# A hybrid encoder trunk on one core: the first mixer's projections read their stationary operand at a step of 8 or 16 bytes

## The chip, the core and the metric

The kernel runs on one core of a Trainium2 chip. A core has a matrix engine (TensorE, in the profile PE, with its weight loads as PEld), a vector engine (DVE), a scalar engine (ACT), GpSimd (POOL), and DMA queues, of which the one on SyncE (SP) carries most loads here. The on-chip memory SBUF has 128 partitions; a tile is 128 partitions by some elements of a row. Matmul results land in PSUM. The metric is the device time of one execution in microseconds. Three runs of the kernel before gave 1371.38, 1371.97 and 1373.08, so the median is 1371.97 us.

## The reference

The input x has 512 tokens of 1024 channels, in float32. Two layers follow each other; each has a token mixer and a gated feed-forward part with a convolution, both between RMS norms. Layer 0's mixer, which the change touches, has one input projection that feeds two groups of heads, retention and neighbourhood attention:

```python
def retention_na_mixer(hn, w_in, ...):
    proj = hn @ w_in
    R, N = RET_WIDTH, NA_WIDTH          # 512, 512
    rq, rk, rv, rg, nq, nk, nv = jnp.split(proj, [R, 2*R, 3*R, 4*R, 4*R + N, 4*R + 2*N], axis=-1)
    ...
    return jnp.concatenate([ret_out, na_out], axis=-1) @ w_out
```

`hn` is 512 x 1024 and `w_in` 1024 x 3584. Layer 1's mixer is a state-space scan (`ssd_mixer`) and is not touched, nor are the two feed-forward parts.

## The kernel before

**Products in three parts.** Each float32 product is made of three matmuls on fp32r operands. ACT rounds an operand to its high part (line 107), DVE subtracts it from the original to get the low part (line 108), and `mm3` adds high x high, high x low and low x high in PSUM (lines 116 to 118). In a row such as `mm<-xh,wlo`, the tile before the comma is the moving operand and the one behind it the stationary operand.

**The first mixer's projections.** `mixer0` walks over four pairs of heads. For each pair, the table `PAIRS` lists the steps; the five steps rq, rk, nq, nk and rg are projections, which go through `project` (the function inside `mixer0`, lines 711 to 733) to `proj_fm` (line 127). The result is feature-major: 128 features of the pair on the partitions, 512 tokens along the row. The stationary operand is therefore a piece of the weight, 128 input channels by 128 features, and the moving operand is `xh` or `xl`, 128 input channels by 512 tokens. One projection runs over KD = 8 key tiles of 128 input channels, so it has 8 x 3 = 24 products, and the four pairs have 4 x 5 x 24 = 480.

**The weights' way.** `wunit` (line 83) fetches one projection's weights as a tile of 128 x 1024 float32 with one DMA of 512 KB on SP (line 76), and casts and subtracts it as a whole. The host lays the array out beforehand: `_cols` (line 1340) puts, for partition p, the eight key tiles one behind the other, 128 features each. `wunit` hands the high and the low tile on as two halves of 512 columns, and `proj_fm` takes key tile k as the 128 neighbouring columns from k % 4 * 128 in half k // 4. `proj_fm` is used by the second mixer's projections too.

**The order around it.** The scheduler keeps the program's order on each engine, and lifts the weight casts ahead of it. On PE, pair 0's five projections come first, in one run. Pair p + 1's projections are then woven into pair p's attention steps, which are short matmuls: scores of 256 moving columns (lines 780, 781, 831, 832), transposes of 128 columns (lines 756, 848), states (line 766) and values (lines 793, 797, 858). Pair 1's projections thus start among pair 0's score matmuls and end ahead of pair 1's key transpose (line 756).

**Two other places that the prediction reads.** In the second mixer, line 1122 has matmuls of 128 moving columns that follow each other with a fresh stationary tile each. Line 985 is a copy on ACT from PSUM into the tile `etot`, 128 x 64 x 4, whose view `p h (i c) -> p c i h` has the 64 heads h innermost; a step from one h to the next is four elements, 16 bytes. Line 1004 is a copy of the same size into `tok`, where h is contiguous.

Of the kernel before, what the change touches and what calls it, by code (L numbers as in the profile page):

```python
# [17 lines left out]
P = 128  # L18
S = 512
NT = S // P  # L20
D = 1024
KD = D // P
# [8 lines left out]
class Env:  # L31
# [92 lines left out]
                self.tc.add_manual_dep(m.ins, i.ins.name, mybir.DependencyInfo(  # L124
                    mybir.DependencyClass.Sync, mybir.DependencyReason.DATA))

    def proj_fm(self, out, w, c0=0, c1=S):

        for k in range(KD):
            hi, lo = w[k // 4]  # L130
            c = slice(k % 4 * P, k % 4 * P + P)
            self.mm3(out[:, c0:c1], hi[:, c], lo[:, c],
                     self.xh[:, k, c0:c1], self.xl[:, k, c0:c1], k == 0, k == KD - 1)

# [436 lines left out]
def log1p_exp_neg(E, alloc, z):  # L571

    nc = E.nc
    e, s, q, r = (alloc(n) for n in "esqr")
    nc.vector.scalar_tensor_tensor(e, z, -1.0, z, op0=ALU.mult, op1=ALU.min)
    nc.scalar.activation(e, e, AF.Exp)
    nc.vector.tensor_scalar(s, e, 2.0, None, op0=ALU.add)
    nc.vector.reciprocal(s, s)
    nc.vector.tensor_tensor(s, s, e, op=ALU.mult)
    nc.vector.tensor_tensor(q, s, s, op=ALU.mult)  # L580
    nc.vector.tensor_scalar(r, q, 2.0 / 15, 2.0 / 13, op0=ALU.mult, op1=ALU.add)
    for c in (11, 9, 7, 5, 3, 1):
        nc.vector.tensor_tensor(r, r, q, op=ALU.mult)
        nc.vector.tensor_scalar(r, r, 2.0 / c, None, op0=ALU.add)
    nc.vector.tensor_tensor(r, r, s, op=ALU.mult)
    return r


NPAIR = 4
CH = 2 * P  # L590
TOEP = CH + P

# [14 lines left out]
def mixer0(E, w0, w_v, w_fm, tabs, dist_d, logit, gn, bias, w_out, g_post_row, done):  # L607
# [4 lines left out]
    with ExitStack() as ctx:  # L612
# [16 lines left out]
        zg = one.tile([P, 104], F32, name="zg")  # L629
        z, gnt = zg[:, :24], zg[:, 24:24 + NPAIR]  # L630
        nc.sync.dma_start(zg[:, :16], logit.partition_broadcast(P))
        nc.sync.dma_start(zg[:, 16:24 + NPAIR], gn)
        lp = log1p_exp_neg(E, lambda n: one.tile([P, 24], F32, name="lp_" + n), z)
# [13 lines left out]
        for s in range(2):  # L647
            ps = [E.mm.tile([P, 512], F32, name="mm") for _ in range(NT)]
            for u in range(4):
                w = w0.pop(0) if w0 else E.wunit(w_v[s, u])  # L650
                for t in range(NT):
                    tt = slice(t * P, (t + 1) * P)
                    for i in range(2):
                        k = 2 * u + i
# [56 lines left out]
        def project(p, o, nm):  # L711
            i = ("rk", "rq", "rg", "nq", "nk").index(nm)
            w = E.wunit(w_fm[i, p])
            ps = E.mm.tile([P, S], F32, name="mm")
            E.proj_fm(ps, w)
            if i < 2:
                a = E.tmp.tile([P, S], F32, name="ra", tag="tmp")
                b = E.tmp.tile([P, S], F32, name="rb", tag="tmp")
                nc.scalar.activation(a, ps, AF.Copy, scale=1.0 if i else 0.125)
                for j in range(4):  # L720
                    nc.sync.dma_start(b[32 * j:32 * j + 32], a[32 * (j ^ 1):32 * (j ^ 1) + 32])
                nc.gpsimd.tensor_tensor(b, b, rot[:, 1], op=ALU.mult)
                nc.vector.tensor_tensor(a, a, rot[:, 0], op=ALU.mult)
                nc.vector.tensor_tensor(a, a, b, op=ALU.add)
                o[nm] = (twice if i else stack)(nm, a)
                o[nm + "a"] = a
            elif i == 2:
                o[nm] = two.tile([P, S], F32, name=nm)
                nc.scalar.activation(o[nm], ps, AF.Silu)
            elif i == 3:  # L730
                o[nm] = stack(nm, ps.rearrange("p (r b c) -> p b r c", r=8, b=4))
            else:
                o[nm] = twice(nm, ps, 0.125)

        def decays(p, o):
# [11 lines left out]
            for c in range(2):  # L747
                cc = slice(c * CH, c * CH + CH)
                nc.scalar.activation(o["qs"][:, cc], away[:, cc], AF.Exp, scale=lgp[:, 2 * p + 1 - c:2 * p + 2 - c])
# [20 lines left out]
        def ret_scores(p, o, i):  # L770

            o["sd", i] = []
            cc = slice(i * P, i * P + CH)
            for h in range(2):
                ps = E.px.tile([P, 2, CH], F32, name="sc", tag="px")
                m = sd.tile([P, 2, CH], F32, name="sd", tag="sd")
                qt, ql = o["rq"]
# [4 lines left out]
                for j in range(2):  # L782
                    w = nc.vector.tensor_tensor(m[:, j], ps[:, j], o["toep"][h][:, P - j * P:P - j * P + CH], op=ALU.mult)
                o["sd", i].append((m, w))
# [77 lines left out]

        os = [{} for _ in range(NPAIR)]
        for p in range(NPAIR):
            for step in PAIRS[p].split():
                q = p + (step[0] == "+")
                step = step.strip("+")
# [472 lines left out]
def _cols(w):  # L1340

    f = w.shape[1]
    return w.reshape(KD, P, f // P, P).transpose(2, 1, 0, 3).reshape(f // P, P, 1024)


def _rows(w, order=None):

    k, n = w.shape
    w = w.reshape(k // P, P, n // 512, 512)
    if order is not None:  # L1350
        w = w[list(order)]
    return w.reshape(k // 256, 2, P, n // 512, 512).transpose(3, 0, 2, 1, 4).reshape(n // 512, k // 256, P, 1024)
# [9 lines left out]
def _rotary_tables(np):  # L1362
    half = 32
    inv = np.float32(1.0) / np.float32(10000.0) ** (np.arange(half, dtype=np.float32) / np.float32(half))
    ang = np.arange(S, dtype=np.float32)[:, None] * inv[None].astype(np.float32)
    c, s = np.cos(ang).T.astype(np.float32), np.sin(ang).T.astype(np.float32)
    return np.stack([np.concatenate([c, c, c, c]), np.concatenate([-s, s, -s, s])], 1)
# [18 lines left out]
def _layouts(np, i):  # L1386
    a = {"x": i["x"][0]}
    a["norms"] = np.stack([i[n] for n in ("norm_mix_pre", "norm_mix_post", "norm_ffn_pre", "norm_ffn_post")], 1)
    w = i["ab_w_in"][0]
    c = lambda j: w[:, 512 * j:512 * j + 512]  # L1390
    a["ab_v"] = np.stack([_rows(c(2))[0], _rows(c(6))[0]])
    a["ab_fm"] = np.stack([_cols(c(j)) for j in (1, 0, 3, 4, 5)])
    a["ab_rot"] = _rotary_tables(np)
    n, t, q = (np.arange(m, dtype=np.float32) for m in (P, S, TOEP))
    k = n[:, None] + P * np.arange(NT, dtype=np.float32)
    a["ab_dist"] = np.concatenate([q[None] - P - n[:, None], np.tile(np.where(t < CH, CH - t, t - CH + 1), (P, 1)),
                                   np.where(k < CH, CH - 1 - k, k - CH)], 1).astype(np.float32)
    logit = i["ab_ret_decay_logit"][0].reshape(2, 8)
    a["ab_logit"] = logit.reshape(16)
    zp = np.repeat(logit.reshape(2, NPAIR, 2).transpose(2, 1, 0).reshape(2, 2 * NPAIR), 64, 0)  # L1400
    a["ab_gn"] = np.concatenate([zp, i["ab_ret_gn_g"][0].reshape(NPAIR, P).T], 1)
    a["ab_bias"] = _na_bias(np, i["ab_na_rpb"][0])
    a["ab_out"] = _rows(i["ab_w_out"][0], OUT_ORDER)

    w = i["c_w_in"][0]
    wz, wx, wb, wc, wd = w[:, :2048], w[:, 2048:4096], w[:, 4096:4608], w[:, 4608:5120], w[:, 5120:]
    a["c_dt"] = wd.reshape(KD, P, 2 * SSD_H).transpose(1, 0, 2).reshape(P, 512)
    a["c_fm"] = np.stack([np.concatenate([_cols(wb[:, P * g:P * g + P]), _cols(wc[:, P * g:P * g + P]),
                                          _cols(wx[:, 512 * g:512 * g + 512]), _cols(wz[:, 512 * g:512 * g + 512])])
                          for g in range(NG)])  # L1410
    cw = np.concatenate([i["c_conv_w"][0], i["c_conv_b"][0][None]])
    xw, bw, cw = cw[:, :2048].reshape(6, NG, 4, P), cw[:, 2048:2560].reshape(6, NG, 1, P), cw[:, 2560:].reshape(6, NG, 1, P)
    a["c_cw"] = np.concatenate([bw, cw, xw], 2).transpose(3, 1, 2, 0)
    sign = np.repeat(np.array([-1, 1], np.float32), SSD_H)
    a["c_dtc"] = np.tile(np.stack([i["c_dt_bias"][0].reshape(-1), i["c_a_log"][0].reshape(-1), sign], 1), (2, 1))
    d = np.repeat(i["c_d_skip"][0].reshape(4 * NG, 2), 64, 1)
    a["c_cols"] = np.stack([d.T, i["c_norm_g"][0].reshape(4 * NG, P).T], 1)
    a["c_mask"] = np.triu(np.ones((P, P), np.float32))
    a["c_out"] = np.stack([_rows(i["c_w_out"][0][512 * g:512 * g + 512]) for g in range(NG)])

    for l in range(2):
        w = i["ffn_w_up"][l]
        a[f"f{l}_up"] = np.stack([_cols(w[:, s * FFN:(s + 1) * FFN]) for s in range(2)])
        cw = np.concatenate([i["ffn_conv_w"][l], i["ffn_conv_b"][l][None]])
        a[f"f{l}_cw"] = cw.reshape(4, 2, NF, P).transpose(3, 1, 2, 0)
        a[f"f{l}_down"] = _quarters(np, i["ffn_w_down"][l])
    return {n: np.ascontiguousarray(v) for n, v in a.items()}
# [28 lines left out]
```

## Time and profile before

| | |
|---|---|
| median of three runs | 1371.97 us |
| the profiled execution's own time | 1372.97 us |
| its span, first to last instruction | 1371.2 us |
| instructions | 19491 |
| granted TensorE clock over the span | 0.998 |
| DMA, mean over the span | 168 GB/s |

The profile is of one execution. An engine's busy time is the union of its instructions' recorded durations; PE's matmuls overlap each other, and their ends are modelled. In rows of instructions the columns are start (us from the span's start), duration (us), engine, line, operation, output and inputs, shape and count; a bracket behind them names the idle time before the row and what ended it. In rows of groups, the number behind the bar is the busy time in us, then the mean duration of one in ns, then the engine's idle time before them. PE and PEld are two rows of the same engine: a weight load runs beside the matmul before its own.

```profile
PE   7999999999999999999999999999999999999997
PEld 6877777798999888888778788787878899998886
PEclk9999999999999999999999999999999999999999
DMA  7443232126779946654566455174433678994654
```

These are tenths of busy time in 40 equal slices of the span, some 34 us each. The first mixer's projections lie in slices 2 to 7.

### The profile page before, as it was taken

What the parts mean: (1) busy time and instruction counts of PE and PEld (TensorE: products, weight loads), DVE (VectorE), ACT (ScalarE), POOL (GpSimd) and SP (SyncE); (2) the same over time, 40 slices, a digit from 0 to 9 for tenths busy, and PEclk for the clock granted to TensorE, in tenths of its full rate; (3) what the DMA queues carried; (4) which work ended last, traced back from release to release, by engine and by line L of the source; (5) the groups of instructions that cost most, each with busy time, mean ns of one, the idle gap of its engine ahead of it and who ended that gap; (6) DMA issues with size and microseconds to landing.
All of it is one profiled execution on the core that took longest, in us unless ns stands there. A gap on an engine that the chain in (4) does not pass through costs nothing.

```text
span 1371.2 us, 19491 instructions
## 1 busy us (share of the span) xinstructions
PE 1344.3 (98%) x7352; PEld 1136.2 (83%) x7352; DVE 1088.5 (79%) x1524; ACT 815.2 (59%) x1345; POOL 111.5 (8%) x130
## 2 busy tenths in 40 slices
PE   7999999999999999999999999999999999999997
PEld 6877777798999888888778788787878899998886
DVE  7368878696768889697878876898789877888876
ACT  5356667453554566664878778477555455556563
POOL 1001110100111100020000110000010001110000
PEclk9999999999999999999999999999999999999999
DMA  7443232126779946654566455174433678994654
GB/s 298 144 138 99 89 100 93 49 93 218 256 210 233 250 147 193 197 201 128 142 180 194 119 178 179 48 204 110 147 128 127 224 249 214 234 242 131 196 179 145
DMA packets 73471, 229.90 MB, mean 168 GB/s; under 512 B 8352, under 2 KB 9120, under 8 KB 72864
## 3 DMA queue, kind: packets, MB, share of 16 engines
q1 hardware_dynamic: 58320, 167.30, 37.3%
q0 software_dynamic: 7168, 46.14, 13.4%
q10 hardware_dynamic: 7888, 15.21, 4.1%
q8 instruction: 58, 0.95, 0.3%
q14 instruction: 37, 0.30, 0.1%
HBM read 221.01 MB, written 51.64 MB: 199 GB/s over the span
## 4 chain that ended last, share of the span: by engine, by line
PE 83%; ACT 6%; DVE 5%; DMA 3%; issue 2%; POOL 1%; DVEq 0%; SPq 0%; POOLq 0%; ACTq 0%
PE mm L116 23%; PE mm L118 23%; PE mm L117 23%; PE pu L118 2%; PE pu L117 2%; PE pu L116 2%; PE pi L1122 1%; PE st L1071 1%; ACT pb L1101 1%; DMA pb<-pd 1%; PE py L1142 1%; ACT whi L107 1%; DVE wlo L108 1%; DMA wst<-in_c_fm 1%; PE pt L173 1%
## 5 line engine op out<-in xcount | busy, mean ns | idle before, releaser
L116 PE MATMUL mm<-xh,whi 128*128 128x512 f32 (+1 forms) x1024 | 382.5, 374 | 0.8 <-ACT z L1041 0.4
L118 PE MATMUL mm<-xl,whi 128*128 128x512 f32 (+1 forms) x1024 | 381.6, 373 | 1.0 <-DVE xl L108 0.5
L117 PE MATMUL mm<-xh,wlo 128*128 128x512 f32 (+1 forms) x1024 | 381.3, 373 | 1.0 <-DVE wlo L108 1.0
L108 DVE TENSOR_TENSOR wlo<-wst,whi 128x1024 fp32r<-128x1024 f32 (+1 forms) x232 | 280.9, 1216 | 89.9 <-ACT whi L107 88.3
L107 ACT CAST whi<-wst 128x1024 fp32r<-128x1024 f32 (+1 forms) x232 | 239.2, 1035 | 145.8 <-PE mm L117 63.5
L116 PEld LDWEIGHTS mm<-xh,whi 128*128 128x128 f32 x1024 | 192.6, 188 | 35.9 <-issue 2.3
L118 PEld LDWEIGHTS mm<-xl,whi 128*128 128x128 f32 x1024 | 192.2, 188 | 35.6 <-issue 1.3
L117 PEld LDWEIGHTS mm<-xh,wlo 128*128 128x128 f32 x1024 | 192.6, 188 | 34.2 <-DVE wlo L108 1.4
L1101 ACT ACTIVATE pb<-pb,tok 128x128 f32<-128x128 f32 x256 | 80.8, 393 | 9.3 <-DMA pb<-pd 7.9
L507 ACT ACTIVATE cv<-mm,cwt 128x512 f32<-128x512 f32 x56 | 43.5, 777 | 68.8 <-PE mm L118 68.7
L118 PE MATMUL mm<-wlo,ab1h 128*128 128x512 f32 x164 | 64.0, 390 | 0.4 <-DVE wlo L108 0.4
L116 PE MATMUL mm<-whi,ab1h 128*128 128x512 f32 x164 | 64.0, 390 | 0.0
L117 PE MATMUL mm<-whi,ab1l 128*128 128x512 f32 x164 | 63.8, 389 | 0.0
L508 DVE SCALAR_TENSOR_TENSOR cv<-mm,cwt,cv 128x511 f32<-128x511 f32 x56 | 41.7, 745 | 22.2 <-ACT cv L507 22.2
L514 ACT ACTIVATE cv<-cv 128x512 f32<-128x512 f32 x44 | 27.8, 632 | 42.8 <-DVE cv L509 42.8
L1035 DVE SCALAR_TENSOR_TENSOR xf<-mm,cwt,xf 128x511 f32<-128x511 f32 (+1 forms) x64 | 47.6, 745 | 6.2 <-ACT xf L1032 5.8
L274 POOL DMA_DIRECT2D ts<-in_f_down x48 | 30.0, 668 | 261.7 <-PE mm L118 227.7
L509 DVE SCALAR_TENSOR_TENSOR cv<-mm,cwt,cv 128x511 f32<-128x511 f32 x56 | 41.8, 746 | 0.9
L116 PE MATMUL mm<-whi,yh 128*128 128x512 f32 x104 | 40.8, 394 | 1.5 <-DVE xf L1035 1.5
L1154 POOL TENSOR_TENSOR sq<-sq 128x512 f32<-128x512 f32 x11 | 16.7, 1516 | 309.1 <-ACT sq L1148 244.6
L117 PE MATMUL mm<-whi,yl 128*128 128x512 f32 x104 | 41.1, 395 | 0.0
L116 PE MATMUL mm<-whi,xh 128*128 128x512 f32 x104 | 40.7, 398 | 0.0
(359 smaller groups left out, 2919.7 us busy)
## 6 DMA issues: line engine op xcount, KB each, us to landing
wst<-in_f_up SPq DMA_DIRECT2D x80, 512.0 KB
ts<-in_f_down POOLq DMA_DIRECT2D x48, 704.0 KB, 6.2
wst<-in_c_fm SPq DMA_DIRECT2D x40, 512.0 KB
wst<-ts SPq DMA_DIRECT2D x32, 512.0 KB
pb<-pd ACTq DMA_DIRECT2D x29, 512.0 KB
wst<-in_f_down SPq DMA_DIRECT2D x24, 512.0 KB
ts<-ts POOLq DMA_DIRECT2D x16, 704.0 KB, 9.9
wst<-in_ab_fm SPq DMA_DIRECT2D x20, 512.0 KB
```

The source lines that it names most:

```text
L107: first = self.nc.scalar.copy(hi, src)
L108: second = self.nc.vector.tensor_tensor(lo, src, hi.bitcast(F32), op=ALU.subtract)
L116: mm(out, lh, rh, start=first, stop=False)
L117: mm(out, ll, rh, start=False, stop=False)
L118: self.product = mm(out, lh, rl, start=False, stop=last)
L274: out.append(lambda i=i, src=src, j=j, c=c, kw=kw: gp.dma_start(part(ts, i, c), part(src, j, c), **kw))
L507: nc.scalar.activation(o, ps, AF.Identity, scale=w(1), bias=w(3))
L508: nc.vector.scalar_tensor_tensor(o[:, 1:], ps[:, :S - 1], w(0), o[:, 1:], op0=ALU.mult, op1=ALU.add)
L509: nc.vector.scalar_tensor_tensor(o[:, :S - 1], ps[:, 1:], w(2), o[:, :S - 1], op0=ALU.mult, op1=ALU.add)
L514: nc.scalar.activation(g, g, AF.Gelu_apprx_tanh)
L1035: nc.vector.scalar_tensor_tensor(r[:, a], ps[:, b], wc(j), r[:, a], op0=ALU.mult, op1=ALU.add)
L1101: nc.scalar.activation(pb[:, dr, c], pb[:, dr, c], AF.Identity, scale=1.0 - 2 * dr, bias=tok[:, 0, c, dr * H + h:dr * H + h + 1])
```

## The change

The weight array of the first mixer's feature-major projections is reordered on the host, pair by pair, after the table `MIX = (2, 4, 1, 2)`. With an entry m, the columns of m neighbouring key tiles alternate in the row: feature 0 of key tiles 0 to m - 1, then feature 1 of them, and so on. `proj_fm` gets an argument `step`, and takes key tile k as 128 columns at that step, starting at the tile's place in its group. For pairs 0 and 3 the step is 2 elements, 8 bytes; for pair 1 it is 4 elements, 16 bytes; for pair 2 it is 1, as before. The same products are made from the same numbers in the same order. The second mixer calls `proj_fm` without `step`, so with 1.

```diff
-    def proj_fm(self, out, w, c0=0, c1=S):
+    def proj_fm(self, out, w, c0=0, c1=S, step=1):
 
         for k in range(KD):
             hi, lo = w[k // 4]
-            c = slice(k % 4 * P, k % 4 * P + P)
+            a = k % 4 // step * step * P + k % step
+            c = slice(a, a + (P - 1) * step + 1, step)
             self.mm3(out[:, c0:c1], hi[:, c], lo[:, c],
                      self.xh[:, k, c0:c1], self.xl[:, k, c0:c1], k == 0, k == KD - 1)
...
+MIX = (2, 4, 1, 2)
...
-            E.proj_fm(ps, w)
+            E.proj_fm(ps, w, step=MIX[p])
...
     a["ab_fm"] = np.stack([_cols(c(j)) for j in (1, 0, 3, 4, 5)])
+    for p, m in enumerate(MIX):
+        w5 = a["ab_fm"][:, p].reshape(5, P, KD // m, m, P)
+        a["ab_fm"][:, p] = w5.transpose(0, 1, 2, 4, 3).reshape(5, P, KD * P)
```

The lists of instructions on the five engines' queues before and after agree row for row, in operation, tiles, shape and place; only the address patterns of the stationary operands in those 360 products differ.

## The prediction, as recorded before the run

> **What bounds the kernel now.** I read the page's busy times first, then the chain that ended last, then a table of stretches for the first mixer, and last the single instructions of the stretches that the change touches.
>
> ```profile
> PE 1344.3 (98%) x7352; PEld 1136.2 (83%) x7352; DVE 1088.5 (79%) x1524; ACT 815.2 (59%) x1345; POOL 111.5 (8%) x130
> PE 83%; ACT 6%; DVE 5%; DMA 3%; issue 2%; POOL 1%; DVEq 0%; SPq 0%; POOLq 0%; ACTq 0%
> ```
>
> The matmul row is busy for 98% of the span, and 83% of the chain lies on it. The weight loads (PEld) have a row of their own that runs beside it. So a weight load costs nothing until it is longer than the matmul it lies beside, and the whole question is how far that is. The next table cuts the first mixer into the stretches of its four head pairs' projections.
>
> ```profile
> core 0: us, PE busy (x) PEld busy (x) DVE busy (x) ACT busy (x) POOL busy (x), PEclk, DMA share, GB/s
> 58.70:86.00 27.30, 27.30 (x122) 22.37 (x120) 13.32 (x14) 13.25 (x19) 2.57 (x2) 1.00 0.58 201
> 88.90:129.90 41.00, 40.45 (x230) 32.24 (x229) 34.49 (x71) 28.41 (x51) 4.35 (x3) 1.00 0.30 95
> 174.70:213.40 38.70, 38.38 (x213) 30.52 (x213) 32.12 (x65) 26.10 (x50) 4.83 (x3) 1.00 0.30 94
> ```
>
> In each the PE column is the stretch's length or nearly so (40.45 of 41.00 us in pair 1's), and the granted clock is 1.00. Nothing else can hide time that is added to PE here: I count it at its full price.
>
> **What sets the distance between two products.** Three streams of this trace show it, with moving operands of 512, 256 and 128 columns.
>
> ```profile
> 58.77 0.39 PE L116 MATMUL mm<-xh,whi 128*128 128x512 f32 x1
> ...
> 70.33 0.39 PE L116 MATMUL mm<-xh,whi 128*128 128x512 f32 x1
> 70.34 0.19 PEld L117 LDWEIGHTS mm<-xh,wlo 128*128 128x128 f32 x1
> ...
> 70.56 0.39 PE L117 MATMUL mm<-xh,wlo 128*128 128x512 f32 x1
> 70.56 0.19 PEld L118 LDWEIGHTS mm<-xl,whi 128*128 128x128 f32 x1
> ...
> 85.75 0.39 PE L118 MATMUL mm<-xl,whi 128*128 128x512 f32 x1
> ```
>
> Pair 0's 120 products run from 58.77 to 85.75 without a break: 26.98 us over 119 intervals, 226.7 ns each. A matmul's recorded 0.39 us overlaps its successor, so the interval counts, not the duration. The load for the next product starts within 0.01 us of the running product's start and is recorded at 0.19 us.
>
> ```profile
> 348.09 0.28 PE L116 MATMUL pu<-xS,whi 128*128 128x256 f32 x1
> ...
> 350.25 0.28 PE L116 MATMUL mm<-xS,whi 128*128 128x256 f32 x1
> 685.11 1.28 PE L1122 MATMUL pi<-cf,state 128*128 128x128 f32 x10
> 685.11 1.08 PEld L1122 LDWEIGHTS pi<-cf,state 128*128 128x128 f32 x9 [0.24 <-issue]
> ```
>
> With 256 moving columns, 18 intervals take 2.16 us: 120 ns. Between 512 and 256 columns lie 106.7 ns, so a moving column takes 0.417 ns and 13.3 ns are fixed. With 128 columns that would give 67 ns, but nine loads in a row end 1.08 us after the first began, (1.08 - 0.19)/8 = 111 ns apart. That is the loop of the load itself, and it ends last there. A product's interval is therefore the longer of two loops: **226.7 ns for 512 columns, 111 ns for a plain load of 128 columns**. How the load's loop grows with the time per column is read from two widths:
>
> ```profile
> L116 PEld LDWEIGHTS mm<-xh,whi 128*128 128x128 f32 x40 | 7.5, 188 | 1.4
> L858 PEld LDWEIGHTS y<-w,nvt 128*64 128x64 f32 x32 | 1.9, 136 | 0.4 <-ACT w L850 0.2 <-DVE qs L750 0.2
> ```
>
> 64 columns more cost 52 ns, 0.81 ns a column, so 104 of the 111 ns are the 128 columns. If a column takes r times as long, the load's loop is 111 + 104(r - 1). It reaches 226.7 ns at **r = 2.11**. Up to there a longer load is hidden by a 512-column product.
>
> **The change, part by part.** The host's reordering of the weight array moves no byte count: the same 512 KB rows are loaded, cast on ACT and subtracted on DVE as contiguous tiles, and no engine's order of instructions changes. These parts I cost at nothing, whatever surrounds them. What changes is the address step of the stationary operand in 360 of the 480 projection products: 240 at 8 bytes (pairs 0 and 3), 120 at 16 bytes (pair 1). Pair 2 stays as it was.
>
> No stationary operand in this trace has a step, so r is bounded from nearby rows. Below stands r = 1, nothing. One row has an innermost step of 16 bytes on the SBUF side, ACT's copy into etot, beside a plain copy of the same size:
>
> ```profile
> L1004 ACT COPY tok<-pt 128x256 f32<-128x256 f32 x2 | 0.8, 375 | 0.6 <-PE pt L1003 0.6
> L985 ACT COPY etot<-pe 128x256 f32<-128x256 f32 x1 | 0.6, 627 | 0.0
> ```
>
> It takes 252 ns more for 256 elements, 0.98 ns each. It is a write by another engine and a single record, but the nearest price there is: 128 columns at 0.98 ns give 126 ns more, a load loop of 237 ns, and r = 2.2. The moving operand gives a second estimate: at 0.417 ns a column PE reads four neighbouring 4-byte columns, 16 bytes, in 1.67 ns. If every column at a 16-byte step costs such a 16-byte piece of its own, 128 columns take 213 ns, the loop is 111 - 104 + 213 = 220 ns, and r = 2.05. I take **r = 2 at 16 bytes** (a loop of 215 ns), as it lies between nothing and the ACT row, and beside the second estimate; both ends stay for the range. At 8 bytes two columns share a piece and I take r = 1; the bound above is r = 2 there too.
>
> Where does r = 2 show? Not inside pair 1's run of 512-column products: 215 ns against 226.7. It shows where a pair 1 product follows a shorter operation, since its load then lies beside less.
>
> ```profile
> 88.88 0.28 PE L781 MATMUL sc<-rql,rk 128*128 128x256 f32 x1
> 88.99 0.39 PE L116 MATMUL mm<-xh,whi 128*128 128x512 f32 x1
> ...
> 103.52 0.60 PE L848 MATMUL pt<-head,e 128*128 128x128 f32 x4
> 103.87 0.48 PE L117 MATMUL mm<-xh,wlo 128*128 128x512 f32 x1
> ...
> 112.65 0.60 PE L858 MATMUL y<-w,nvt 128*64 128x128 f32 x7
> 113.18 0.50 PE L118 MATMUL mm<-xl,whi 128*128 128x512 f32 x1
> ...
> 129.64 0.39 PE L118 MATMUL mm<-xl,whi 128*128 128x512 f32 x1
> ```
>
> Pair 1's 120 products start between 88.99 and 129.64, woven into pair 0's attention. Going through them in order, ten follow something else: seven a score matmul of 256 columns (L781 or L832, as the first row pair), two a transpose (L848), one the last value product (L858). The seven have a 120 ns loop to hide in: 7 x (215 - 120) = 0.67 us. The three behind short operations pay the whole extra 104 ns: 0.31 us. Sum: **+1.0 us**. PE stands idle 0.55 us in all in that stretch, so little of it is taken back.
>
> Against the profiled execution's own 1372.97 us this gives 1374.0. That execution lies 1.0 us above the median of the three runs, 1371.97; I put the sum on the median: **1373.0 us**.
>
> By the Trainium skill, "SBUF — State Buffer", section "Specifications (TRN2)", SBUF has lines of 16 bytes and wants at least two hits in a line for full bandwidth. By that rule the 8-byte step is free, the 16-byte step pays, and the rule speaks against the change; it names no size, and no run here shows it yet. The sum by it is the one above with some r over 1 for pair 1 alone.
>
> **The rivals.**
>
> *Slower: the 16-byte load outgrows its product.* If each column needs three or four slots, the load's loop is 319 or 423 ns and bounds all of pair 1. At r = 3: 110 x (319 - 226.7) = 10.2 us inside the run, 7 x 199 ns = 1.4 and 3 x 208 ns = 0.6 at the seams, together 12.2 us: 1384.2. At r = 4: 21.6 + 2.1 + 0.9 = 24.7 us: 1396.6. It decides from r = 2.11, and passes 0.2% of the time (2.7 us, about what a measurement of this kernel tells from no change) at a loop of 240 ns, r = 2.24. For it: the ACT row sits at r = 2.2, at the edge. Against it: the ACT row itself gives only 110 x 10.3 ns + 7 x 117 ns + 3 x 126 ns = 2.3 us, 1374.3, still within 0.2%; nothing in the trace shows 3. Chance 0.20.
>
> *The change does nothing: r = 1 at both steps.* Sum 0, 1372.0. For it: the score matmuls L831 and L832 read a moving operand in separate pieces of eight columns, and follow each other at 0.12 to 0.13 us like the contiguous ones above. But that is no step at every column. It lies within 0.2% as the forecast does.
>
> ```profile
> 103.14 0.28 PE L832 MATMUL sc<-nkl,nq 128*128 128x256 f32 x1
> 103.26 0.29 PE L831 MATMUL sc<-nk,nq 128*128 128x256 f32 x1
> 103.39 0.29 PE L832 MATMUL sc<-nkl,nq 128*128 128x256 f32 x1
> ```
>
> *Also the 8-byte step doubles.* Pair 0's unbroken stream hides it; pair 3's stretch has nine seams as pair 1's has ten, so 0.9 us more: 1373.9.
>
> *Loads don't overlap.* If load and product took turns on the array, r = 2 would add 104 ns to each of pair 1's 120 products, 12.5 us: 1384.5. The trace speaks against it: at 256 columns the two in turn would need 104 + 107 = 211 ns, and the interval is 120. The Trainium skill, "TensorE: Matmul & The Clock Gate", section "The mechanism", says that a load overlaps a running matmul only where the row groups differ; the trace disagrees, with full 128-row loads starting 0.01 us after a 128-row matmul. Chance 0.01.
>
> *Faster.* If the fixed 13.3 ns per product came from the two reads meeting in SBUF, and the step parted them, 360 products would save 4.8 us: 1367.2. But it is the same 13.3 ns at 256 columns, where the load lies beside all of the product, so it doesn't grow with the overlap. Chance 0.03.
>
> **How the numbers follow.** The forecast together with its two neighbours that stay within 0.2% (r from 1 to 2.24 for pair 1, up to 2 for the others) has 0.76; within that, r = 2 is likeliest, and its own range, with 0.7 us of spread between runs below and the ACT row above, is 1371.2 to 1374.8. Slower has 0.20 + 0.01 = 0.21, of which I give r = 3 or less (and the turns) 0.13 and more than that 0.08. Faster has 0.03. The range starts at 1371.0 and must reach past the r = 3 price of 1384.2 to leave out less than 2 in 10: up to 1386. Left out are r = 4 and the faster case, 0.11.
>
> **What would show it.** The recorded load of pair 1 (projections of rq, rk, nk, nq, rg after 88.99) should grow from 188 to about 290 ns, those of pairs 0 and 3 stay at 188. The interval inside pair 1's run should stay at 226.7 ns, and its stretch grow from 41.0 to 42.0 us. An interval over 226.7 there, 240 or 320, would make the forecast wrong and name r at once; a load interval over 226.7 in pair 0's stretch would make the 8-byte step the cause. Loads still at 188 ns with the same stretches would mean that the step costs nothing.

## The result and the profile after

| | before | changed |
|---|---|---|
| median, us (18 runs each) | 1372.02 | 1374.45 |
| lowest to highest | 1370.46 to 1374.46 | 1372.30 to 1376.84 |
| ratio | | 1.0016, 95% interval 1.0009 to 1.0023 |

The change costs some 2.2 us (1.2 to 3.2 by the interval), clear of zero, and about the 0.2% that the prediction called no change. The forecast was 1.0 us more.

First the page's busy times and its chain, then the table of stretches of the changed kernel.

```profile
PE 1348.6 (98%) x7352; PEld 1145.9 (84%) x7352; DVE 1088.2 (79%) x1524; ACT 814.7 (59%) x1345; POOL 112.7 (8%) x130
PE 89%; DVE 5%; ACT 3%; issue 1%; DMA 1%; POOL 1%; DVEq 0%; SPq 0%; POOLq 0%; ACTq 0%
```

```profile
60.30:88.40 28.10, 28.10 (x122) 23.18 (x122) 14.21 (x16) 14.58 (x22) 2.99 (x2) 1.00 0.56 195
89.40:131.90 42.50, 42.23 (x230) 38.89 (x229) 34.54 (x71) 28.40 (x51) 4.39 (x3) 1.00 0.30 94
176.70:215.90 39.20, 38.97 (x213) 31.17 (x213) 32.28 (x65) 26.26 (x50) 4.82 (x3) 1.00 0.31 93
```

The columns are as before: stretch, its length, then busy times of PE, PEld, DVE, ACT and POOL. All three stepped pairs have longer stretches, pair 0 (27.3 to 28.1) and pair 3 (38.7 to 39.2) too, which the prediction had at nothing. PEld's own time in pair 1's stretch goes from 32.2 to 38.9 us. The weight loads' groups say how much one load grew. The three rows are of pair 0, pair 1 and pair 3, one line of the products each.

```profile
L116 PEld LDWEIGHTS mm<-xh,whi 128*128 128x128 f32 x40 | 7.7, 193 | 1.6
L116 PEld LDWEIGHTS mm<-xh,whi 128*128 128x128 f32 x40 | 12.5, 312 | 0.0
L116 PEld LDWEIGHTS mm<-xh,whi 128*128 128x128 f32 x40 | 7.7, 194 | 1.5 <-issue 0.2
```

At 16 bytes a load is recorded at 312 ns instead of 188, at 8 bytes at 193. Now the intervals, from the first and last instructions of two unbroken runs: pair 0's and pair 1's last one in the changed kernel, then pair 1's last one before.

```profile
60.36 0.39 PE L116 MATMUL mm<-xh,whi 128*128 128x512 f32 x1
...
88.13 0.39 PE L118 MATMUL mm<-xl,whi 128*128 128x512 f32 x1
...
114.96 0.40 PE L116 MATMUL mm<-xh,whi 128*128 128x512 f32 x1
...
131.65 0.39 PE L118 MATMUL mm<-xl,whi 128*128 128x512 f32 x1
```

```profile
113.52 0.39 PE L116 MATMUL mm<-xh,whi 128*128 128x512 f32 x1
...
129.64 0.39 PE L118 MATMUL mm<-xl,whi 128*128 128x512 f32 x1
```

Pair 0's 119 intervals take 27.77 us, **233.3 ns** each (226.7 before). The last 72 products of pair 1 follow each other without a break, 71 intervals in 16.69 us, **235.1 ns** each; before, the same 71 took 16.12 us (227.1). So the interval moved at both steps, where the forecast had it stay. The seams (the places where a product follows some other operation) pay too, for instance the first one and one behind a transpose; the second of the next two fences has that transpose's seam in the kernel before.

```profile
89.39 0.28 PE L783 MATMUL sc<-rql,rk 128*128 128x256 f32 x1
89.50 0.51 PE L116 MATMUL mm<-xh,whi 128*128 128x512 f32 x1
...
104.89 0.60 PE L850 MATMUL pt<-head,e 128*128 128x128 f32 x4
105.25 0.60 PE L117 MATMUL mm<-xh,wlo 128*128 128x512 f32 x1
105.69 0.40 PE L118 MATMUL mm<-xl,whi 128*128 128x512 f32 x1
```

```profile
103.87 0.48 PE L117 MATMUL mm<-xh,wlo 128*128 128x512 f32 x1
104.19 0.40 PE L118 MATMUL mm<-xl,whi 128*128 128x512 f32 x1
```

A product that waits for its weights is recorded as longer, not as later: 0.51 instead of 0.39 us and 0.60 instead of 0.48 us, 0.12 us more each. The operation behind it then starts later: 0.44 us after the product instead of 0.32 in the rows of the transpose's seam. Over all ten seams of pair 1 the interval behind the product grew from 2.58 to 3.73 us in sum.

What does not show in the time is pair 0's 0.8 us. These are the key transpose and the first score product behind pair 0's run, before and then changed.

```profile
86.56 0.66 PE L756 MATMUL pt<-head,ra 128*128 128x128 f32 x4 [0.43 <-DVE ra L724]
88.42 0.39 PE L780 MATMUL sc<-rq,rk 128*128 128x256 f32 x1 [1.20 <-DVE rk L685]
```

```profile
88.36 0.60 PE L758 MATMUL pt<-head,ra 128*128 128x128 f32 x4
88.92 0.39 PE L782 MATMUL sc<-rq,rk 128*128 128x256 f32 x1
```

Before, PE waited 0.43 and 1.20 us there for DVE, which makes the keys; in the changed kernel it doesn't wait. A longer run of pair 0 eats into that wait, but the wait fell by 1.6 us and the run grew by 0.8 only. The experiments take up the rest.

### The profile page after: what moved, and what is told of

Its sections match the earlier page's. It is cut to its first block, busy times and chain, and to the rows that moved or that the text cites. A ratio compares the mean times of both kernels' runs of the same rounds, so it can differ in the third digit from the quotient of the medians.

```text
span 1371.8 us, 19491 instructions
## 1 busy us (share of the span) xinstructions
PE 1348.6 (98%) x7352; PEld 1145.9 (84%) x7352; DVE 1088.2 (79%) x1524; ACT 814.7 (59%) x1345; POOL 112.7 (8%) x130
## 4 chain that ended last, share of the span: by engine, by line
PE 89%; DVE 5%; ACT 3%; issue 1%; DMA 1%; POOL 1%; DVEq 0%; SPq 0%; POOLq 0%; ACTq 0%
PE mm L116 24%; PE mm L118 24%; PE mm L117 24%; PE pu L118 2%; PE pu L117 2%; PE pu L116 2%; PE pi L1124 2%; PE st L1073 2%; PE py L1144 1%; DVE wlo L108 1%; PE pt L1017 1%; PE pt L174 1%; PE y L799 1%; DVE xs L165 1%; ACT junk L154 0%
## 5 line engine op out<-in xcount | busy, mean ns | idle before, releaser
L116 PEld LDWEIGHTS mm<-xh,whi 128*128 128x128 f32 x1024 | 198.0, 193 | 34.6 <-issue 2.5
L118 PEld LDWEIGHTS mm<-xl,whi 128*128 128x128 f32 x1024 | 197.6, 193 | 34.2 <-issue 1.3
L117 PEld LDWEIGHTS mm<-xh,wlo 128*128 128x128 f32 x1024 | 198.0, 193 | 33.1 <-DVE wlo L108 1.6
```

The costliest lines, as they stand in the source:

```text
L116: mm(out, lh, rh, start=first, stop=False)
L117: mm(out, ll, rh, start=False, stop=False)
L118: self.product = mm(out, lh, rl, start=False, stop=last)
```

## The experiments

**Which pair costs what.** Four kernels differ from the changed one in the table `MIX` alone.

```diff
-MIX = (2, 4, 1, 2)
+MIX = (2, 1, 1, 2)    # only_8
+MIX = (1, 4, 1, 1)    # only_16
+MIX = (2, 2, 2, 2)    # all_8
+MIX = (4, 4, 4, 4)    # all_16
```

> Pairs 0 and 3 at 8 bytes as in the changed kernel, pair 1 back at neighbouring columns. Theory A (both steps cost, 8 bytes 6.7 ns per product in a run of 512-column products): pair 0's run of 119 intervals takes 27.8 us instead of 27.0, pair 3's intervals rise from 227 to 233 ns (stretch +0.5 us), pair 1's stay at 227; the time rises by 0.5 us if the wait for the keys behind pair 0 hides its part, by 1.3 if not. Rival B (the prediction's step: 8 bytes is free and all of the 2.4 us is pair 1's): the time is that of the kernel before within 0.3 us.

> Pair 1 at 16 bytes as in the changed kernel, pairs 0 and 3 back at neighbouring columns. Theory A: pair 1's stretch of 40.65 us takes 1.5 us more, from the ten seams (some 0.12 us each) and 110 intervals of 235 instead of 230 ns; the time rises by 1.5 us. Rival B: all of the 2.4 us is here. Rival C (the prediction's sum): the intervals inside the run stay at 227 and only the seams pay, 1.0 us.

> All four pairs at 8 bytes. Theory A: intervals of 233 instead of 227 ns in all four pairs' runs, some 450 of them, 3.0 us of PE work; the time rises by 2 to 3 us, less what the wait behind pair 0 hides. Rival B: no change.

> All four pairs at 16 bytes. Theory A: pair 0's unbroken run rises to a mean of 235 ns, +1.0 us, and the other three pairs pay 1.5 us each at their ten, nine and nine seams and inside their runs: the time rises by 5 to 6 us. Rival C (seams only): pair 0 pays nothing and the sum is 3.0 us.

Measured, with the stretches of each profile beside the time. A pair's stretch runs from the start of its first product to that of its last; pair 0's is given to pair 1's first product, since the wait lies in it. "Whole" is from pair 0's first to pair 3's last product.

| kernel | ratio (95% interval) | pair 0 run | pair 0 to pair 1 | pair 1 | pair 3 | whole |
|---|---|---|---|---|---|---|
| before | 1 | 26.97 | 30.22 | 40.65 | 38.37 | 154.36 |
| changed | 1.0016 (1.0009 to 1.0023) | 27.77 | 29.14 | 42.15 | 38.84 | 155.25 |
| only_8 | 1.0001 (0.9992 to 1.0010) | 27.77 | 29.54 | 40.69 | 38.86 | 154.18 |
| only_16 | 1.0014 (1.0005 to 1.0023) | 26.97 | 30.23 | 42.13 | 38.35 | 155.80 |
| all_8 | 1.0007 (0.9998 to 1.0016) | 27.77 | 29.63 | 41.19 | 38.84 | 155.32 |
| all_16 | 1.0028 (1.0017 to 1.0039) | 27.97 | 29.69 | 42.13 | 39.70 | 157.95 |

Pair 1 at 16 bytes costs 1.5 us wherever it is set, and only_16's 1.0014 is 1.9 us (0.7 to 3.2): the largest part of the change. Pair 3 at 8 bytes costs 0.5 us on PE. The rows of pair 3's last run in only_8, and of pair 1 in only_16:

```profile
196.74 0.39 PE L117 MATMUL mm<-xh,wlo 128*128 128x512 f32 x1
...
214.47 0.39 PE L118 MATMUL mm<-xl,whi 128*128 128x512 f32 x1
```

```profile
90.46 0.51 PE L116 MATMUL mm<-xh,whi 128*128 128x512 f32 x1
...
132.60 0.39 PE L118 MATMUL mm<-xl,whi 128*128 128x512 f32 x1
```

The two rows of only_8 lie 76 intervals apart, 17.73 us, 233.3 ns each: so 8 bytes is not free in the run. In the time of only_8 that is lost (1.0001), because pair 0's 0.8 us is hidden and 0.5 us is less than the interval resolves. all_8 rose by 1.0 us (-0.3 to 2.2): on PE its pairs 1, 2 and 3 pay 0.5 us each and pair 0's 0.8 us is hidden. all_16 rose by 3.8 us, less than the 5 to 6 expected: its pairs 2 and 3 pay 1.3 us each and pair 0's 1.0 us is hidden. Rival B of only_8 and all_8 (8 bytes free) is refuted by the intervals of the products; the times alone would allow it. Rival C (the seams alone pay) is refuted by the intervals in only_16, and in all_16 by pair 0's run, which has no seam and grew from 26.97 to 27.97 us.

**What sets the interval.** A kernel with no network in it, only blocks of 32 products, each with one step and one width.

```python
def block(name, step, n, m=P, count=32):
    ps = mm.tile([P, S], F32, name=name, tag="mm")
    for k in range(count):
        w = (wa, wb)[k % 2]
        nc.tensor.matmul(ps[:m, :n], columns(w, step, k // 3, m), mv[:, k % 2 * 512:k % 2 * 512 + n],
                         start=k == 0, stop=k == count - 1)
    ...
```

> This kernel leaves the network out: it runs 21 blocks of 32 fp32r products each (a first one of 40 at step 1), with the stationary columns at a step of 1, 2, 3, 4 or 8 elements (4 to 32 bytes) and 512, 256 or 128 moving columns, then steps 1, 2, 4 with only 64 stationary columns. The changed kernel's profile has 226.7 ns between products at step 1, 233.3 at step 2, and 231 to 240 (mean 235) at step 4, all with 512 moving columns; its loads are recorded at 188, 193 and 309 ns. Theory A (a fixed part of each product grows at 8 bytes, the load's own loop binds at 16): step 1 gives 227, 120 and at 128 columns what the shorter of the two lets through (67 to 111); step 2 gives 233, 127 and at most 118; step 4 gives about 235 at all three widths, since the load is the bound whatever it lies beside; step 8 elements the same 235, step 3 between. Rival B (the fixed part grows at both steps and no load binds): step 4 gives 235 at 512 but 213.3 to 106.7 less, 128, at 256. Rival C (the load's reads meet the matmul's reads, so that the extra goes with the number of loaded columns): with 64 stationary columns the extra of step 2 over step 1 is half, 3.3 ns, where A says 6.7 as before.

Mean interval in ns over each block's last 25, from the starts of its matmuls. In the 512-column blocks at 16 and 32 bytes the granted clock dipped to 0.5 at the start; their means, marked *, are over the last 20 intervals, behind the dip.

| step | 512 columns | 256 | 128 |
|---|---|---|---|
| 4 bytes | 226.6 | 120.0 | 111.6 |
| 8 | 233.3 | 120.0 | 117.8 |
| 12 | 235.6 | 176.2 | 175.2 |
| 16 | 235.0* | 233.4 | 233.6 |
| 32 | 244.2* | 240.8 | 240.2 |

Two rows each of the 16-byte blocks with 256 and with 128 columns, 24 intervals apart:

```profile
78.15 0.40 PE L37 MATMUL s4n<-mv,wb 128*128 128x256 f32 x1
...
83.75 0.40 PE L37 MATMUL s4n<-mv,wb 128*128 128x256 f32 x1
...
85.56 0.40 PE L37 MATMUL s4n<-mv,wb 128*128 128x128 f32 x1
...
91.17 0.43 PE L37 MATMUL s4n<-mv,wb 128*128 128x128 f32 x1
```

5.60 us and 5.61 us: 233 and 234 ns. At a 16-byte step the interval is the same at 256 and 128 columns, so there it is the load's own loop: theory A's second half holds at these widths, and rival B, which had 128 ns at 256 columns, is out. At 12 bytes it is 175. The first half of theory A fell: at 8 bytes and 256 columns the interval is 120.0 and not 127, so no fixed part grew. Rival C fell as well: with 64 stationary columns and 512 moving ones the interval is 230.0 at a 4-byte step (over the 22 intervals behind a dip of the clock) and 231.6 at 8 bytes, 1.6 ns more, where C had 3.3 and A 6.7.

From 8 to 16 bytes the load's loop goes with the number of 16-byte pieces that its columns touch. 128 columns touch 64 pieces at a step of 8 bytes, 96 at 12 and 128 at 16; by the table's last column a piece takes 1.84, 1.83 and 1.83 ns, an estimate from these blocks. (The plain load touches 32 pieces and takes 111.6 ns, so something else bounds it.) 64 columns at 16 bytes touch 64 pieces again, and their products with 256 moving columns follow each other at 117.8 ns, as those of 128 columns at 8 bytes with 128 moving columns do. The rows are of two blocks: 12 bytes with 512 moving columns, 25 intervals apart, and those 64 columns, the first and the last product, 31 intervals apart.

```profile
50.18 0.40 PE L37 MATMUL s3n<-mv,wa 128*128 128x512 f32 x1
...
56.07 0.39 PE L37 MATMUL s3n<-mv,wb 128*128 128x512 f32 x1
...
146.93 0.28 PE L37 MATMUL h4n<-mv,wa 128*64 128x256 f32 x1
...
150.59 0.28 PE L37 MATMUL h4n<-mv,wb 128*64 128x256 f32 x1
```

At 512 columns the load's loop does not explain the interval. It is 233.3 ns at 8 bytes and 235.6 at 12, though the loads' loops there are 118 and 175 ns, and 233.3 with 64 columns at 16 bytes, whose loads need 118 at most. So it is not shown that the 235 ns of pair 1's run come from its load's 233.

> This kernel leaves the network out: blocks of 24 fp32r products (a first one of 40), at steps of 1 and 2 elements with 512, 480, 448, 384, 320, 288, 256 and 192 moving columns, then with 64 stationary columns (512 and 384 moving), then step 1 from a start that is not a multiple of 16 bytes (512 and 256), then 96 stationary columns (512). In the first such kernel step 2 took 233.3 against 226.7 ns at 512 columns, but 120.0 against 120.0 at 256. Theory T (an interval is a whole number of ticks of 6.7 ns, the work rounded up): every mean is a multiple of 6.7, and step 2 costs one tick at some widths and none at others. Rival P (the 8-byte step costs in proportion to the moving columns over 256): the extra rises evenly, 0 at 256, 1.7 at 320, 3.3 at 384, 5.8 at 480. Rival L (the 8-byte step lengthens the load by 6 ns and it shows wherever the load ends last): no extra at 320 and above, where the load has room.

Mean over each block's last 17 intervals, in ns, with the moving columns across:

| step | 512 | 480 | 448 | 384 | 320 | 288 | 256 | 192 |
|---|---|---|---|---|---|---|---|---|
| 4 bytes | 226.6 | 216.4 | 202.9 | 173.4 | 146.6 | 131.8 | 119.6 | 111.6 |
| 8 bytes | 233.4 | 216.5 | 203.5 | 173.4 | 146.8 | 133.2 | 120.0 | 118.6 |

```profile
18.66 0.39 PE L39 MATMUL s1n<-mv,wa 128*128 128x512 f32 x1
...
23.87 0.39 PE L39 MATMUL s1n<-mv,wb 128*128 128x512 f32 x1
24.10 0.39 PE L39 MATMUL s2n<-mv,wa 128*128 128x512 f32 x1
...
29.47 0.40 PE L39 MATMUL s2n<-mv,wb 128*128 128x512 f32 x1
...
102.24 0.39 PE L39 MATMUL o<-mv,wa 128*128 128x512 f32 x1
...
107.56 0.39 PE L39 MATMUL o<-mv,wb 128*128 128x512 f32 x1
```

These are the first and last products of three blocks at 512 columns, 23 intervals each: neighbouring columns 5.21 us (226.5 ns), 8 bytes 5.37 us (233.5), and neighbouring columns from a start off the 16-byte grid 5.32 us (231.3). All three theories fell. The extra of 8 bytes isn't proportional (P: nothing at 480, 384 and 320), isn't only a load that ends last (L: it is there at 512, though it shows at 192 columns too, where the load does end last), and the means are no whole ticks of 6.7 ns (T: 216.4, 202.9, 131.8). With 64 stationary columns the 512-column interval was 230.0 at neighbouring columns and 231.5 at 8 bytes, with 96 neighbouring columns 230.1. So 226.7 at 512 columns is a low value that, of the forms tried, only 128 neighbouring columns from an aligned start reach. The start is not what the 8-byte step pays for: half of its products begin on the 16-byte grid, and every interval of that block is 233 or 234 ns. Why stays open.

**Is pair 0's part hidden, and by what?** In the profiles so far the sum from pair 0 to pair 1 was even shorter where pair 0 was stepped. I took the cause to be DVE and GpSimd meeting: before, GpSimd's second multiplication and DVE's addition start 0.02 us apart.

```profile
79.94 1.29 POOL L722 TENSOR_TENSOR rb<-rb,rot 128x512 f32<-128x512 f32 x1 [1.76 <-DMA rb<-ra]
```

```profile
79.96 1.81 DVE L724 TENSOR_TENSOR ra<-ra,rb 128x512 f32<-128x512 f32 x1
```

The addition takes 1.81 us there and 0.69 in the changed kernel, where the multiplication comes later. Four more runs tested it; the diff is in `MIX` alone again, (1, 4, 1, 2) for pair0_plain and (2, 1, 1, 1) for pair0_8.

> The changed kernel with pair 0 back at neighbouring columns (pair 1 at 16 bytes, pair 3 at 8). Theory A (pair 0's longer run is given back, because it keeps DVE's addition of the rotated queries, line 726, ahead of GpSimd's second multiplication, line 724, so that the keys come earlier): pair 0's run falls from 27.8 to 27.0 us, but the addition meets the multiplication again and takes 1.8 instead of 0.7 us, and from pair 0's first product to pair 1's it is 30.2 us again instead of 29.1; the time doesn't fall and may rise by 0.5 us against the changed kernel. Rival (pair 0's 0.8 us is on the path): the time falls by 0.8 us against the changed kernel.

> Only pair 0 at 8 bytes. Theory A: its run is 27.8 instead of 27.0 us, the addition of line 726 takes 0.7 instead of 1.8 us, and from pair 0's first product to pair 1's it is 29.1 to 29.7 us against 30.2 before; the time is 0.5 to 1 us under the kernel before, too little to tell in these rounds. Rival (pair 0's 0.8 us is on the path): 0.8 us over it, and 31.0 us to pair 1's first product.

> The changed kernel once more, for a second profile and a time in these rounds: 1.5 to 2.5 us over the kernel before, with the intervals of its first profile (233 in pair 0's run, 231 to 240 in pair 1's) and 29.1 to 29.7 us from pair 0's first product to pair 1's, whatever the start of pair 0 is.

> The kernel before once more, for a second profile: no change in time, intervals of 227 in all four pairs' runs, the addition of the rotated queries at 1.8 us and 30.2 us from pair 0's first product to pair 1's. If the addition takes 0.7 us here, theory A's account of pair 0 rests on chance between executions.

| kernel | ratio (95% interval) | pair 0 run | pair 0 to pair 1 | DVE's addition, us | whole |
|---|---|---|---|---|---|
| pair0_plain | 1.0014 (1.0003 to 1.0024) | 26.97 | 29.39 | 0.69 | 155.49 |
| pair0_8 | 1.0000 (0.9991 to 1.0009) | 27.77 | 29.55 | 0.69 | 153.60 |
| changed_again | 1.0012 (1.0002 to 1.0021) | 27.77 | 29.74 | 0.69 | 155.79 |
| before_again | 0.9995 (0.9986 to 1.0005) | 26.97 | 29.39 | 0.69 | 153.53 |

Half of theory A fell. In before_again, the same kernel as before, the addition came first by 0.02 us and took 0.69 us; GpSimd's multiplication then took 1.83:

```profile
81.42 0.69 DVE L724 TENSOR_TENSOR ra<-ra,rb 128x512 f32<-128x512 f32 x1
```

```profile
81.44 1.83 POOL L722 TENSOR_TENSOR rb<-rb,rot 128x512 f32<-128x512 f32 x1 [0.67 <-DMA rb<-ra]
```

With pair 0 plain it is a draw between executions, worth 0.83 us (30.22 against 29.39), and the stepped pair 0 is not what avoids it alone: it is avoided in two of the four profiles with pair 0 plain, and in all six with pair 0 stepped, where the multiplication starts 0.14 to 0.87 us behind the addition. The other half holds: with pair 0 stepped, the way to pair 1's first product takes 29.14 to 29.74 us in six profiles, mean 29.55, against 29.39 to 30.23 in the four with pair 0 plain. Against the two plain profiles where the addition came first, 29.39 us both, the 0.8 us of PE work add 0.16 us on the mean and 0.35 at most. The rival, 31.0 us to pair 1's first product, is out by these stretches. The times agree, as pair0_plain is no faster than changed_again, but their intervals of more than 1 us each way would not settle 0.8 us alone.

## Why the prediction came out

- **The forecast, within 0.2% of the time before, held in the number**: 1.0016, and 1374.45 us in the range 1371.0 to 1386.0. The size was 2.2 us (1.2 to 3.2) where 1.0 was forecast. The mechanism held in part: loads overlap products, a 16-byte step lengthens the load, the seams pay for it, and a wait hides pair 0. It failed inside the runs. By the prediction's own sign, an interval over 226.7 ns in pair 1's run, that step was wrong. The number held even so because what it left out was small: 0.6 us in pair 1's run and 0.5 in pair 3's, beside 2.7 us for the 0.2%. Nothing in the prediction said that it would be; that is luck.
- **"I take r = 2 at 16 bytes (a loop of 215 ns)"**: too low. The load's loop measured 233.4 ns, against 111.6 for the plain load, which by the prediction's formula is r = 2.17. The nearest row, ACT's copy into etot with r = 2.2 and a loop of 237 ns, was almost exact, though nothing shows that the two share a cause. I went below the row, towards the argument from the moving operand. That argument priced a 16-byte piece at 1.67 ns, and the loops give 1.83; the 7 ns that it adds for the rest are not seen.
- **"It shows where a pair 1 product follows a shorter operation"**: right. With a loop of 233.4 ns the prediction's sum for the ten seams is 7 x 113 + 3 x 122 ns = 1.16 us, and the intervals behind them grew by 1.15 (2.58 to 3.73). PE's idle time in the stretch, a wait ahead of a transpose, gave 0.27 us of it back (0.55 to 0.27), so the part with the seams rose by 0.9 us (24.5 to 25.5).
- **"Not inside pair 1's run of 512-column products"**: wrong. The 71 unbroken intervals took 0.57 us more (16.12 to 16.69). Pair 1 as a whole cost 1.5 us instead of 1.0. The ACT row's sum, 2.3 us, priced each product in the run at 10.3 ns, and 8 were measured, for a reason that stays open.
- **"At 8 bytes two columns share a piece and I take r = 1"**: the load's loop is indeed nearly the plain one (117.8 against 111.6 ns at 128 columns, 120.0 in both at 256), yet the interval at 512 columns rose to 233.3. The term that failed is the 226.7 ns itself: I treated it as a property of 512 columns that holds until a load takes longer. Pair 3 paid 0.5 us, pair 0 0.8.
- **"Pair 0's unbroken stream hides it"**: for another reason than given. The stream did grow; the wait for the keys behind it took it up.
- **The rivals.** Slower by r = 3 or 4 is out, as is the change doing nothing. That the 8-byte step doubles the load is out by its loop of 117.8 ns. Loads in turn with products are out too: at 16 bytes and 256 columns turns would need some 213 + 107 = 320 ns, and 233 were measured. Faster is out.
- **The rule of the Trainium skill**, "SBUF — State Buffer", section "Specifications (TRN2)", two hits in a 16-byte line for full bandwidth: it gave the right order (8 bytes hardly longer loads, 12 bytes 175, 16 bytes 233). By that rule alone pairs 0 and 3 would have paid nothing, and at 512 columns they paid 6.7 ns a product.

Added up from the profiles: 1.5 us (pair 1), 0.5 (pair 3) and up to 0.2 (pair 0) make 2.0 to 2.2 us, beside 2.2 (1.2 to 3.2) and 1.6 (0.3 to 2.9, changed_again) by the times. In single profiles the draw of 0.83 us lies over this: from pair 0's first to pair 3's last product it is 155.25 and 155.79 us changed, 154.36 and 153.53 before.

## What to carry to other kernels

A load whose own loop is longer than the product beside it sets the pace, so find both loops in the trace before pricing a slower load: here 112 ns plain and 233 ns at a 16-byte step, beside 227 for 512 moving columns and 120 for 256. The reverse does not hold to the last per cent: a load that fitted by a wide margin (118 ns) still cost 6.7 ns a product at 512 columns, so an interval measured with one form of operand need not hold for another. Here the nearest measured row, another engine's, came closer than an argument about rates; that is one case. Count the places where the neighbour is short, and look for a wait behind the lengthened run that takes the loss up.

## What the runs showed of the hardware that was not expected

- The interval of fp32r products with 512 moving columns is 226.7 ns, of the forms tried, only for 128 neighbouring stationary columns that start on a 16-byte boundary. At an 8-byte step it was 233.4, from a start off that boundary 231.5, with 96 or 64 stationary columns 230. At 384 and 320 columns the 8-byte step made no difference (173.4, 146.6 against 146.8).
- A load's loop at steps of 4, 8, 12, 16 and 32 bytes was 112, 118, 175, 234 and 240 ns for 128 columns: from 8 to 16 bytes some 1.83 ns for each 16-byte piece touched, and from 16 to 32 bytes little more.
- When DVE adds two tiles in SBUF while GpSimd multiplies two, the one that starts second pays: 1.81 instead of 0.69 us for DVE, or 1.83 instead of 1.29 for GpSimd, decided by 0.02 us between executions of one program. The Trainium skill, "SBUF — State Buffer", section "Who interferes with whom", says that a DVE instruction with two SBUF inputs contends with a GpSimd instruction that reads SBUF and that issue order decides who blocks; these rows agree.
